# Another order of seven block products, one weight-sum buffer, and the first products on an unnormalised x, in the MLPs of a two-layer trunk

## The chip, the cores and the metric

The kernel runs on one core of a Trainium2 chip. The metric is the device time of one execution in microseconds.

## What is computed

A trunk of two layers on x (512 tokens, width 1024), all in fp32. Layer 0 mixes tokens by windowed attention, layer 1 by a recurrent block; both add a cross-attention on a memory. Each layer ends in the MLP that the change is about:

```python
x = x + jnp.concatenate([mixed, mo], axis=-1) @ w_out[l]
x = x + squared_relu_mlp(rms_norm(x, mlp_norm[l]), w_up[l], w_down[l])
# rms_norm:          x * rsqrt(mean(x*x) + EPS) * g
# squared_relu_mlp:  square(relu(h @ w_up)) @ w_down      (w_up 1024x4096, w_down 4096x1024)
```

## The kernel before, in words

x lies transposed in SBUF (xT, eight tiles of 128 features by 512 tokens). A product of fp32 values is made of three matmuls on high and low halves: high·high, high·low, low·high (L407, L409, L411). Each weight tile of 128x1024 comes as `raw` from memory (SP's queue, L102), ScalarE casts it to the high half `wh` (L352) and VectorE subtracts to get the low half `wl` (L353). There are four buffers each of wh and wl.

`mlp(l)` (L427) treats the hidden width in four groups of 1024. A step u*g* makes one group of w_up's product, a step d*g* takes one group through w_down and adds the result to xT. The order is u0 u1 d0 u2 d1 u3 d2, then d3 in layer 0; layer 1 ends with a plain product instead (`emit_last`). Each step is a 2x2 block product made with seven block products instead of eight (`seven`, L391), in the order of `PRODUCTS`. A step works on two quads (halves of the output blocks); for each product and quad there are 24 matmuls of 128x256, so a step has 336.

The weight operands of the seven products are blocks a11, a12, a22 and sums of them (`Quad.operand`, L333). The sums s3 and s1 are formed by a second, accumulating DMA from POOL's queue into a raw tile (L328). VectorE adds a22 to s3 into a tile `wsum` (L343, for product 6) and later a12 to it (L346, for product 3). Raw and wsum tiles of a Quad share a ring of RAWS = 8 buffers (a12, and a11 in the first step, use two others). The activation operands (`factor`, L368) are blocks of the input or sums of them, split into halves (L135, L136; for product 6 L378, L379) and kept in `h7` (seven buffers, made once for all u steps) or `u7` (two buffers, d steps). The results of products are added up in three PSUM banks per quad: x takes products 1, 6, 5, 3, y takes 2, z takes 7 and 4. In a d step VectorE adds each result from its bank to xT (L488), in a u step ScalarE and VectorE form the outputs and their squared ReLU (L458 to L473).

At the start of `mlp` the squares of x are summed while w_out's last products still run (`add_square`), then TensorE sums over partitions (`ps_ss`, L169), VectorE and ScalarE form 1/rms (L173 to L178), VectorE spreads it on a diagonal (`dg`, L158), TensorE broadcasts it (`ps_bc`, L160), and VectorE writes x·g/rms into blocks b (L439), from which the factors come.

Each engine runs its instructions in one fixed order. A scheduler sets it when the program is built, from the order of the code and the priorities given by `ahead(n)`; buffers that come free set the waits.

Of the kernel before, what the change touches and what calls it, by code (L numbers as in the profile page):

```python
# [60 lines left out]
def trunk(ctx: ExitStack, tc, xT_d, memT_d, wts_d, cols_d, ident_d, mask_d, pos_d, sink_d, outT_d, out_d, order):  # L61
# [302 lines left out]
    def activations(pool, room, tag, b, bufs):  # L364

        b[0] = room.tile([128, 4, 256], F32, tag="b0", name="b0", bufs=1)

        def factor(i, fine=False):  # L368
            t = pool.tile([128, 2, 4, 256], F32R, tag=tag, name=tag, bufs=bufs)
            src = b[{1: 11, 6: 0, 7: 12, 5: 11, 3: 22, 2: 21, 4: 0}[i]]  # L370
            with ahead(AHEAD_T):
                if i == 4:
                    V.tensor_tensor(out=b[0], in0=b[0], in1=b[21], op=ALU.subtract)
                for k in (((0, 2), (2, 4)) if i == 1 else ((0, 4),)):
                    k = slice(*k)
                    h, l, x = t[:, 0, k], t[:, 1, k], src[:, k]
                    if i == 6:
                        A.activation(out=h, in_=x, func=AF.Copy, scale=-1.0)  # L378
                        V.scalar_tensor_tensor(out=l, in0=x, scalar=-1.0, in1=h.bitcast(F32), op0=ALU.mult,  # L379
                                               op1=ALU.subtract)  # L380
                    else:
                        split((h, l), x)
# [8 lines left out]
    def seven(quads, factor, taken):  # L391
# [3 lines left out]
        for i in PRODUCTS:  # L395
            t = factor(i)
            for q, w in enumerate(quads):
                wh, wl = w.operand(i)
                if i in (1, 2, 7):
                    {1: x, 2: y, 7: z}[i][q] = seven_bank()  # L400
# [1 line left out]
                for p in range(2):
                    out = bank[:, p * 256:(p + 1) * 256]
                    for k in range(4):
                        c = slice((p * 4 + k) * 128, (p * 4 + k + 1) * 128)
                        first, last = i in (1, 2, 7) and p == 0 and k == 0, p == 1 and k == 3
# [552 lines left out]
```

## Time and profile before

| | |
|---|---|
| median of 3 runs | 1252.86 us (1249.09 to 1253.36) |
| profiled execution | 1252.73 us, span 1251.0 us |
| TensorE busy | 1177.0 us, 94% of the span |
| VectorE busy | 997.6 us, 80% |
| ScalarE busy | 767.4 us, 61% |
| mean granted TensorE clock | 0.969 |

The table is read from the top: the profiled execution is one of the same kind as the runs, its span is the time from its first to its last instruction, and the engines' busy times lie beside each other in it. Busy times over the whole span say little of one stage; the rows further below are of single stages.

### The profile page before, as it was taken

What the parts mean: (1) busy time and instruction counts of PE and PEld (TensorE: products, weight loads), DVE (VectorE), ACT (ScalarE), POOL (GpSimd) and SP (SyncE); (2) the same over time, 40 slices, a digit from 0 to 9 for tenths busy, and PEclk for the clock granted to TensorE, in tenths of its full rate; (3) what the DMA queues carried; (4) which work ended last, traced back from release to release, by engine and by line L of the source; (5) the groups of instructions that cost most, each with busy time, mean ns of one, the idle gap of its engine ahead of it and who ended that gap; (6) DMA issues with size and microseconds to landing.
All of it is one profiled execution on the core that took longest, in us unless ns stands there. A gap on an engine that the chain in (4) does not pass through costs nothing.

```text
span 1251.0 us, 20268 instructions
## 1 busy us (share of the span) xinstructions
PE 1177.0 (94%) x8084; PEld 1079.9 (86%) x8084; DVE 997.6 (80%) x1425; ACT 767.4 (61%) x1199; POOL 53.4 (4%) x69
## 2 busy tenths in 40 slices
PE   6999999996998999998999999999789999989997
PEld 6888888875898999998998877777589999989997
DVE  7978999766768968978987679997678687886954
ACT  7684598734665565574456789883377646646632
POOL 0000000001000100010000000001000100011000
PEclk9999999996998999998989999999799999999999
DMA  7412101125765677577233122238045676667131
GB/s 251 156 52 84 68 34 35 51 100 136 216 184 152 160 215 184 163 194 202 52 124 112 59 93 84 102 113 236 22 152 160 178 203 176 177 138 218 51 102 68
DMA packets 48910, 164.44 MB, mean 131 GB/s; under 512 B 5552, under 2 KB 9008, under 8 KB 48816
## 3 DMA queue, kind: packets, MB, share of 16 engines
q1 hardware_dynamic: 39456, 130.90, 30.8%
q0 software_dynamic: 8640, 31.46, 14.0%
q8 instruction: 63, 1.03, 0.3%
q10 hardware_dynamic: 720, 0.79, 0.2%
q14 instruction: 31, 0.25, 0.1%
HBM read 161.04 MB, written 2.10 MB: 130 GB/s over the span
## 4 chain that ended last, share of the span: by engine, by line
PE 66%; DVE 18%; DMA 8%; ACT 5%; issue 3%; SPq 0%; DVEq 0%; POOLq 0%; ACTq 0%
PE ps L409 10%; PE ps L411 10%; PE ps L407 10%; DMA raw<-wts 8%; DVE wl L353 4%; PE ps_o L118 3%; PE ps_o L119 3%; PE ps_o L120 3%; DVE xT L488 2%; PE sc L712 2%; PE pt L732 1%; DVE wl L114 1%; ACT wh L352 1%; PE pv L118 1%; PE ps_mq L119 1%
## 5 line engine op out<-in xcount | busy, mean ns | idle before, releaser
L407 PE MATMUL ps<-h,wh 128*128 128x256 f32 x896 | 251.6, 282 | 13.8 <-ACT h L135 11.5
L411 PE MATMUL ps<-h,wl 128*128 128x256 f32 x896 | 250.6, 281 | 4.5 <-DVE wl L353 4.5
L409 PE MATMUL ps<-h,wh 128*128 128x256 f32 x896 | 251.3, 281 | 1.7 <-DVE h L136 1.7
L352 ACT CAST wh<-raw 128x1024 fp32r<-128x1024 f32 x150 | 156.5, 1048 | 149.3 <-PE ps L409 129.8
L409 PE MATMUL ps<-u,wh 128*128 128x256 f32 x784 | 225.1, 287 | 10.3 <-DVE u L379 6.5
L407 PE MATMUL ps<-u,wh 128*128 128x256 f32 x784 | 224.2, 286 | 10.2 <-DVE xT L488 9.4
L411 PE MATMUL ps<-u,wl 128*128 128x256 f32 x784 | 223.9, 286 | 1.2 <-DVE wl L353 1.2
L353 DVE TENSOR_TENSOR wl<-raw,wh 128x1024 fp32r<-128x1024 f32 x150 | 182.1, 1219 | 46.8 <-ACT wh L352 46.4
L407 PEld LDWEIGHTS ps<-h,wh 128*128 128x128 f32 x896 | 171.4, 192 | 18.1 <-ACT h L135 15.1
L411 PEld LDWEIGHTS ps<-h,wl 128*128 128x128 f32 x896 | 170.3, 191 | 5.1 <-DVE wl L353 5.1
L409 PEld LDWEIGHTS ps<-h,wh 128*128 128x128 f32 x896 | 171.0, 191 | 2.5 <-DVE h L136 2.5
L407 PEld LDWEIGHTS ps<-u,wh 128*128 128x128 f32 x784 | 154.0, 197 | 11.2 <-DVE xT L488 10.0
L409 PEld LDWEIGHTS ps<-u,wh 128*128 128x128 f32 x784 | 153.3, 196 | 11.8 <-DVE u L379 7.1
L411 PEld LDWEIGHTS ps<-u,wl 128*128 128x128 f32 x784 | 153.0, 195 | 1.6 <-DVE wl L353 1.6
L113 ACT CAST wh<-raw 128x1024 fp32r<-128x1024 f32 x88 | 92.2, 1047 | 67.9 <-DMA raw<-wts 19.2
L114 DVE TENSOR_TENSOR wl<-raw,wh 128x1024 fp32r<-128x1024 f32 x88 | 107.1, 1217 | 24.5 <-ACT wh L113 24.2
L328 POOL DMA_DIRECT2D raw<-wts x60 | 52.0, 867 | 1103.0 <-DMA raw<-wts 850.1
L352 ACT CAST wh<-wsum 128x1024 fp32r<-128x1024 f32 x60 | 62.6, 1049 | 58.2 <-PE ps L409 52.2
L353 DVE TENSOR_TENSOR wl<-wsum,wh 128x1024 fp32r<-128x1024 f32 x60 | 72.9, 1220 | 23.1 <-ACT wh L352 22.8
L343 DVE TENSOR_TENSOR wsum<-raw 128x1024 f32<-128x1024 f32 x30 | 36.7, 1223 | 47.1 <-DMA raw<-wts 33.7
L488 DVE TENSOR_TENSOR xT<-xT,ps 128x512 f32<-128x512 f32 x98 | 66.0, 679 | 1.9 <-PE ps L411 1.5
L472 ACT ACTIVATE b<-b 128x512 f32<-128x512 f32 x48 | 30.1, 630 | 43.5 <-DVE b L470 43.5
(276 smaller groups left out, 2677.2 us busy)
## 6 DMA issues: line engine op xcount, KB each, us to landing
raw<-wts SPq DMA_DIRECT2D x238, 512.0 KB, 3.7
raw<-wts POOLq DMA_DIRECT2D x60, 512.0 KB, 7.7
mraw<-memT SPq DMA_DIRECT2D x16, 128.0 KB, 4.1
xT<-xT SPq DMA_DIRECT2D x8, 256.0 KB, 4.8
outT<-xT SPq DMA_DIRECT2D x8, 128.0 KB, 1.8
out<-fo ACTq DMA_DIRECT2D x2, 256.0 KB, 2.5
out<-fo SPq DMA_DIRECT2D x2, 256.0 KB, 2.7
posi<-pos SPq DMA_DIRECT2D x1, 256.0 KB, 5.6
```

Source lines behind the costliest of these rows:

```text
L113: A.copy(out=h, in_=raw)
L114: V.tensor_tensor(out=l, in0=raw, in1=h.bitcast(F32), op=ALU.subtract)
L118: T.matmul(out, lhsT=lhsT[0], rhs=rhs[0], start=start, stop=False)
L119: T.matmul(out, lhsT=lhsT[0], rhs=rhs[1], start=False, stop=False)
L120: T.matmul(out, lhsT=lhsT[1], rhs=rhs[0], start=False, stop=stop)
L328: P.dma_start(out=t, in_=wts_d[fetch_n[0]], accum_op=ALU.add)
L352: A.copy(out=h, in_=raw)
L353: V.tensor_tensor(out=l, in0=raw, in1=h.bitcast(F32), op=ALU.subtract)
L407: T.matmul(out, lhsT=wh[:, c], rhs=t[:, 0, k], start=first, stop=False, skip_group_check=True)
L409: T.matmul(out, lhsT=wh[:, c], rhs=t[:, 1, k], start=False, stop=False, skip_group_check=True)
L411: T.matmul(out, lhsT=wl[:, c], rhs=t[:, 0, k], start=False, stop=last, skip_group_check=True)
L488: V.tensor_tensor(out=dst, in0=dst, in1=src, op=ALU.add if n < 20 else ALU.subtract)
```

## The change

Products 7 and 6 change places. The tile s3 is kept as one sum `s`, to which a22 is added in place ahead of product 6 and a12 ahead of product 3; there is no wsum tile, and RAWS is 6. The factor sums are made each with its factor, u7 has three buffers, and the separate priority of the first step's weights (AHEAD_F) is gone. In u0 products 1 and 2 run on x·g without 1/rms: their operands `hx` take two of the h7 buffers and are made as soon as a tile of xT is done. Their results are multiplied by 1/rms (bc) afterwards: product 1's copies `p1` at L477, then added into the outputs (L486), products 1 and 2's sum at L513. x·g/rms is still written for the other factors, in 16 halves (L455) instead of 8 whole rows, and dg lies in b0's room.

```diff
-RAWS = 8
+RAWS = 6
-PRODUCTS = (1, 2, 6, 7, 5, 3, 4)
+PRODUCTS = (1, 2, 7, 6, 5, 3, 4)
...
         def operand(self, i):
             a = self.a
-            with ahead(AHEAD_F if self.first and i not in (1, 2) else AHEAD_W):
+            with ahead(AHEAD_W):
                 if i == 1:
                     a[11] = self.load((0, 0))
                 elif i == 2:
-                    a[12], a["s3"] = self.load((0, 1)), self.load((0, 0), (1, 0))
+                    a[12], a["s"] = self.load((0, 1)), self.load((0, 0), (1, 0))
+                elif i == 7:
+                    a[22] = self.load((1, 1))
                 elif i == 6:
-                    a[22], a["s1"] = self.load((1, 1)), self.load((1, 0), (1, 1))
-                    a["n"] = self.pool.tile([128, 1024], F32, tag="raw", name="wsum")
-                    V.tensor_tensor(out=a["n"], in0=a["s3"], in1=a[22], op=ALU.add)
-                op = split_raw(a[{1: 11, 6: "n", 7: "s3", 5: "s1", 3: "n", 2: 12, 4: 22}[i]])
-                if i == 6:
-                    V.tensor_tensor(out=a["n"], in0=a["n"], in1=a[12], op=ALU.add)
-            return op
+                    a["s1"] = self.load((1, 0), (1, 1))
+                if i in (6, 3):
+                    V.tensor_tensor(out=a["s"], in0=a["s"], in1=a[22 if i == 6 else 12], op=ALU.add)
+                return split_raw(a[{1: 11, 6: "s", 7: "s", 5: "s1", 3: "s", 2: 12, 4: 22}[i]])
...
-                if i == 1:
-                    V.tensor_tensor(out=b[11], in0=b[11], in1=b[12], op=ALU.subtract)
-                    V.tensor_tensor(out=b[0], in0=b[22], in1=b[11], op=ALU.add)
-                    V.tensor_tensor(out=b[12], in0=b[22], in1=b[12], op=ALU.subtract)
+                if i in (7, 6, 5, 4):
+                    t, x, y, op = {7: (12, 22, 12, ALU.subtract), 6: (0, 12, 11, ALU.add), 5: (11, 0, 22, ALU.subtract),
+                                   4: (0, 0, 21, ALU.subtract)}[i]
+                    V.tensor_tensor(out=b[t], in0=b[x], in1=b[y], op=op)
...
+    def product(i, quad, t, bank, start=None):
...
-    def seven(quads, factor, taken):
+    def seven(quads, factor, taken, left=False):
-        for i in PRODUCTS:
+        for i in PRODUCTS[2 if left else 0:]:
...
+            with ahead(AHEAD_E):
+                plain = [hm.tile([128, 2, 4, 256], F32R, tag="h7", name="hx", bufs=7) for _ in range(2)]
             for c in range(KD):
+                with ahead(AHEAD_E):
+                    split_scaled(part(plain[c % 2], c // 2), xT[c][:, :256], col(C_MLP + 8 * l + c))
                 add_square(acc, xT[c], c == 0)
             bc = st.tile([128, S], F32, tag="bc", name="bc", bufs=1)
-            rstd_of(acc, S, bc)
-            for c in (0, 2, 4, 6, 1, 3, 5, 7):
-                two = [a.rearrange("p (t s) -> p t s", t=2) for a in (xT[c], bc)]
-                V.scalar_tensor_tensor(out=b[c % 2 + 1][:, :, c // 2], in0=two[0], scalar=col(C_MLP + 8 * l + c),
-                                       in1=two[1], op0=ALU.mult, op1=ALU.mult)
+            first = [Quad(rp, f"w_up{l}", 0, q * 4, True) for q in range(2)]
+            sums, start = [], []
+            for q in range(2):
+                start.append(seven_bank())
+                product(1, first[q], plain[0], start[q])
+                sums.append(st.tile([128, S], F32, tag="sq", name="p1"))
+                with ahead(AHEAD_E):
+                    A.copy(out=sums[q], in_=start[q])
+            room = up.tile([128, 4, 256], F32, tag="b0", name="dg", bufs=1)
+            rstd_of(acc, S, bc, dg=room.rearrange("p a b -> p (a b)")[:, :S].rearrange("p (a b) -> p a b", a=4))
+            for q in range(2):
+                product(2, first[q], plain[1], start[q], False)
...
+            def normalise(half):
+                with ahead(AHEAD_T + 100 * half):
+                    for c in range(KD):
+                        V.scalar_tensor_tensor(out=b[c % 2 + 1][:, half, c // 2], in0=xT[c][:, HALVES[half]],
+                                               scalar=col(C_MLP + 8 * l + c), in1=bc[:, HALVES[half]], op0=ALU.mult,
+                                               op1=ALU.mult)
...
                 if g == 0:
-                    for i in PRODUCTS:
+                    normalise(1)
+                    h_of(7)
+                    normalise(0)
+                    for i in (6, 1, 5):
+                        h_of(i)
+                    with ahead(AHEAD_T):
+                        r = bc[:, :256].rearrange("p (o t) -> p o t", o=1).to_broadcast([128, 2, 256])
+                        two = [a.rearrange("p (a t) -> p a t", a=2) for a in sums + start]
+                        for q in range(2):
+                            V.tensor_tensor(out=two[q], in0=two[q], in1=r, op=ALU.mult)
+                    for i in (3, 4, 2):
                         h_of(i)
...
+                    if g == 0 and i in (6, 5, 3):
+                        dst = b[{6: 21, 5: 22, 3: 12}[i]][:, k]
+                        V.tensor_tensor(out=dst, in0=bank, in1=two[q], op=ALU.add)
...
+                if g == 0:
+                    for q in range(2):
+                        u = b[11][:, q * 2:q * 2 + 2]
+                        V.scalar_tensor_tensor(out=u, in0=two[q + 2], scalar=0.0, in1=r, op0=ALU.max, op1=ALU.mult)
+                        A.activation(out=u, in_=u, func=AF.Square)
+                quads = first if g == 0 else [Quad(rp, f"w_up{l}", 0, g * 8 + q * 4) for q in range(2)]
+                seven(quads, h_of, taken, g == 0)
...
-                      activations(up, up, "u7", us.pop(g), 2), taken)
+                      activations(up, up, "u7", us.pop(g), 3), taken)
```

TensorE's order at the start of layer 0's MLP, before: w_out's last matmuls, the two of the 1/rms chain, then product 1 on normalised operands (h7).

```order
L119 MATMUL ps_o_2886<-o1_2003,wh_2868 128x512
L120 MATMUL ps_o_2886<-o1_2003,wl_2869 128x512
L169 MATMUL ps_ss_2939<-ones_76,acc_2915 128x1 x4
L160 MATMUL ps_bc_2958<-dg_2953,ones_76 128x512
L407 MATMUL ps_7_3005<-h7_2970,wh_3001 128x256
L407 MATMUL ps_7_3037<-h7_2970,wh_3033 128x256
L409 MATMUL ps_7_3005<-h7_2970,wh_3001 128x256
```

And now: the last rows of product 1's start and of product 2, on hx, around the two matmuls of the 1/rms chain, up to the first row of product 7.

```order
L394 MATMUL ps_7_2990<-hx_2916,wh_2993 128x256
L395 MATMUL ps_7_2990<-hx_2916,wh_2993 128x256
L396 MATMUL ps_7_2990<-hx_2916,wl_2994 128x256
L169 MATMUL ps_ss_3024<-ones_76,acc_2915 128x1 x4
L394 MATMUL ps_7_2990<-hx_2916,wh_2993 128x256
...
L395 MATMUL ps_7_2990<-hx_2917,wh_3083 128x256
L160 MATMUL ps_bc_3042<-dg_3023,ones_76 128x512
L396 MATMUL ps_7_2990<-hx_2917,wl_3084 128x256
...
L396 MATMUL ps_7_2990<-hx_2917,wl_3084 128x256
L394 MATMUL ps_7_3161<-h7_3120,wh_3164 128x256
```

27 product matmuls now stand ahead of ps_ss, 56 between it and ps_bc, and 13 behind that before the first matmul on normalised operands.

VectorE's order in layer 1 at the end of d1, before: the xT adds of product 5 (two per quad: banks 10817 and 11032, then 10849 and 11061), the splits (wl) of product 4's weights, and between them the sum for the next step, u3 (wsum).

```order
L488 TENSOR_TENSOR xT_79<-xT_79,ps_7_10817 128x2x256
L353 TENSOR_TENSOR wl_11215<-raw_10951,wh_11214 128x1024
L488 TENSOR_TENSOR xT_79<-xT_79,ps_7_11032 128x2x256
L343 TENSOR_TENSOR wsum_11417<-raw_11340,raw_11412 128x1024
L488 TENSOR_TENSOR xT_79<-xT_79,ps_7_10849 128x2x256
L353 TENSOR_TENSOR wl_11244<-raw_10988,wh_11243 128x1024
L488 TENSOR_TENSOR xT_79<-xT_79,ps_7_11061 128x2x256
L488 TENSOR_TENSOR xT_79<-xT_79,ps_7_10817 128x2x256
L136 TENSOR_TENSOR u7_11210<-b0_10802,u7_11210 128x1024
```

And now the same place (banks 10860, 10969 and 11000), and the first rows in which the next step's sums are added.

```order
L352 TENSOR_TENSOR wl_11233<-raw_10970,wh_11232 128x1024
L528 TENSOR_TENSOR xT_79<-xT_79,ps_7_10969 128x2x256
L528 TENSOR_TENSOR xT_79<-xT_79,ps_7_10860 128x2x256
L375 TENSOR_TENSOR b0_11747<-b1_10368 128x1024
L528 TENSOR_TENSOR xT_79<-xT_79,ps_7_11000 128x2x256
L352 TENSOR_TENSOR wl_11262<-raw_11001,wh_11261 128x1024
...
L352 TENSOR_TENSOR wl_11434<-raw_11359,wh_11433 128x1024
L345 TENSOR_TENSOR raw_11359<-raw_11359,raw_11431 128x1024
L352 TENSOR_TENSOR wl_11465<-raw_11396,wh_11464 128x1024
L345 TENSOR_TENSOR raw_11396<-raw_11396,raw_11462 128x1024
```

The a22 add (L345) of u3 now stands behind the splits of u3's own product 7 (wl_11434, wl_11465), each quad by itself; between the two splits of d1's product 4 there is only a sum of factors (L375) and xT adds.

SP's queue around the start of layer 0's MLP, before: w_out's last raw tile, then the MLP's. The wait of raw_3065 is for w_out's last matmul.

```order
L102 DMA raw_2866<-wts 128x1024 [waits DMAHW6_49,DVE_49]
L102 DMA raw_2999<-wts 128x1024 [waits DMAHW7_49,DVE_49]
L102 DMA raw_3031<-wts 128x1024 [waits DMAHW0_49,DVE_49]
L102 DMA raw_3063<-wts 128x1024 [waits DMAHW1_49,DVE_49]
L102 DMA raw_3100<-wts 128x1024 [waits DMAHW2_49,DVE_49]
L102 DMA raw_3065<-wts 128x1024 [waits PE_49]
L102 DMA raw_3102<-wts 128x1024
```

And now. The wait of raw_3047 is for the end of windowed attention (its last split, on VectorE, and matmul), those of raw_2958 and raw_2991 for the splits of w_out's last two tiles.

```order
L101 DMA raw_2866<-wts 128x1024 [waits DMAHW6_49,DVE_49]
L101 DMA raw_3047<-wts 128x1024 [waits DVE_49,PE_49]
L101 DMA raw_2958<-wts 128x1024 [waits DMAHW7_49,DVE_49]
L101 DMA raw_3080<-wts 128x1024
L101 DMA raw_3162<-wts 128x1024
L101 DMA raw_3193<-wts 128x1024
L101 DMA raw_2991<-wts 128x1024 [waits DMAHW0_49,DVE_49]
```

The first load in the MLP's ring no longer waits for w_out's last matmul.

## Rows read from the trace of the kernel before

**Rows 1.** The page: busy time of TensorE (share of the span, instructions), and by engine the shares of the chain that ended last.

```profile
PE 1177.0 (94%) x8084; PEld 1079.9 (86%) x8084; DVE 997.6 (80%) x1425; ACT 767.4 (61%) x1199; POOL 53.4 (4%) x69
PE 66%; DVE 18%; DMA 8%; ACT 5%; issue 3%; SPq 0%; DVEq 0%; POOLq 0%; ACTq 0%
```

**Rows 2.** Busy time of each engine in single block steps: the window (us from the span's start) and its length, then PE, PEld, DVE, ACT and POOL busy us (instructions), granted TensorE clock, share of the DMA engines, GB/s. In order: layer 0 u0, d0, d1, d2, d3; layer 1 u0, d0, u2, d1, d2.

```profile
294.62:342.88 48.26, 43.71 (x336) 42.61 (x337) 39.81 (x41) 29.79 (x40) 2.59 (x3) 0.91 0.56 148
381.20:427.51 46.31, 42.18 (x339) 41.59 (x337) 40.48 (x43) 24.57 (x28) 3.45 (x4) 0.93 0.64 177
467.08:510.88 43.80, 41.17 (x339) 40.97 (x337) 37.02 (x40) 22.16 (x24) 3.45 (x4) 0.96 0.66 170
548.96:596.00 47.04, 42.07 (x339) 41.65 (x337) 41.91 (x50) 25.58 (x33) 4.01 (x5) 0.93 0.72 188
596.00:636.50 40.50, 39.28 (x339) 38.47 (x338) 38.31 (x42) 21.46 (x22) 0.31 (x1) 1.00 0.23 63
899.97:945.77 45.80, 41.37 (x336) 40.28 (x337) 35.87 (x37) 28.19 (x38) 2.59 (x3) 0.95 0.48 142
985.38:1032.42 47.04, 42.95 (x339) 42.54 (x337) 40.59 (x43) 24.46 (x28) 3.45 (x4) 0.93 0.61 167
1032.42:1070.50 38.08, 38.08 (x339) 38.08 (x337) 27.98 (x28) 24.87 (x33) 3.45 (x4) 1.00 0.68 182
1070.50:1116.01 45.51, 40.94 (x339) 40.43 (x337) 38.91 (x42) 22.63 (x25) 4.31 (x5) 0.96 0.67 172
1155.58:1195.15 39.57, 39.57 (x338) 39.57 (x337) 38.11 (x45) 24.85 (x30) 0.86 (x1) 1.00 0.23 67
```

**Rows 3.** Waits of VectorE, TensorE and SP's queue over the whole span: who waited at which line for whom, us in total, times, longest.

```profile
DVE wsum L343 <- DMA raw<-wts: 33.7, 11, 6.8
PE ps L407 <- DVE xT L488: 9.4, 3, 4.6
PE ps L409 <- DVE u L379: 6.5, 3, 3.0
SPq L102 <- DVE wsum L346: 296.3, 30, 42.1
```

**Rows 4.** Timeline of layer 1 at d1's product 3, which follows product 5 in the same banks: start, duration (us), engine, line, operation, and the idle time before it with what ended it.

```profile
1098.08 0.68 DVE L488 TENSOR_TENSOR xT<-xT,ps 128x512 f32<-128x512 f32 x1
1098.14 0.28 PE L407 MATMUL ps<-u,wh 128*128 128x256 f32 x1
...
1101.09 0.28 PE L411 MATMUL ps<-u,wl 128*128 128x256 f32 x1
...
1104.05 1.23 DVE L343 TENSOR_TENSOR wsum<-raw 128x1024 f32<-128x1024 f32 x1 [5.29 <-DMA raw<-wts]
...
1105.93 0.58 PE L407 MATMUL ps<-u,wh 128*128 128x256 f32 x1 [4.56 <-DVE xT L488]
```

**Rows 5.** Timeline of layer 0 from w_out's last matmul to the first product; columns as in rows 4 (SPq: six DMA issues one after the other).

```profile
277.25 0.40 PE L120 MATMUL ps_o<-o,wl 128*128 128x512 f32 x1
277.68 2.84 SPq L102 DMA_DIRECT2D raw<-wts  x6
...
291.31 1.23 DVE L343 TENSOR_TENSOR wsum<-raw 128x1024 f32<-128x1024 f32 x1 [6.82 <-DMA raw<-wts]
...
294.62 0.79 PE L407 MATMUL ps<-h,wh 128*128 128x256 f32 x2 [7.94 <-ACT h L135]
```

**Rows 6.** The same stretch in layer 1.

```profile
887.83 0.39 PE L120 MATMUL ps_o<-ol,wl 128*128 128x512 f32 x1
...
890.25 0.68 DVE L149 TENSOR_TENSOR acc<-acc,sq 128x512 f32<-128x512 f32 x1
...
890.99 1.87 PE L169 MATMUL ps_ss<-ones,acc 128*128 128x1 f32 x8 [2.77 <-DVE acc L149]
...
894.13 0.87 DVE L158 TENSOR_SCALAR dg<-ident,r 128x128 f32<-128x128 f32 x4
...
899.97 0.80 PE L407 MATMUL ps<-h,wh 128*128 128x256 f32 x2 [2.77 <-ACT h L135]
```

**Rows 7.** Busy times as in rows 2, of the end of w_out in layer 0 and of the two stretches at half clock.

```profile
255.00:277.60 22.60, 22.60 (x99) 18.23 (x98) 14.28 (x18) 8.61 (x12) 0.00 (x0) 1.00 0.19 70
279.85:300.32 20.47, 9.15 (x33) 7.25 (x34) 11.22 (x23) 2.58 (x5) 3.63 (x4) 0.50 0.93 241
890.83:904.48 13.65, 7.95 (x27) 6.02 (x28) 8.43 (x20) 2.17 (x5) 0.00 (x0) 0.50 0.00 0
```

**Rows 8.** Groups of instructions by line: engine, operation, output and inputs, count, busy us, mean ns of one, idle us before.

```profile
L353 DVE TENSOR_TENSOR wl<-raw,wh 128x1024 fp32r<-128x1024 f32 x150 | 182.1, 1219 | 46.8 <-ACT wh L352 46.4
L140 DVE SCALAR_TENSOR_TENSOR memH<-mraw,cols,memH 128x256 fp32r<-128x256 f32 x16 | 7.0, 479 | 0.7 <-ACT memH L139 0.6
L139 ACT ACTIVATE memH<-mraw,cols 128x256 fp32r<-128x256 f32 x16 | 7.1, 498 | 0.7 <-DMA mraw<-memT 0.5
L352 ACT CAST wh<-raw 128x1024 fp32r<-128x1024 f32 x150 | 156.5, 1048 | 149.3 <-PE ps L409 129.8 <-PE ps_o L119 9.3 <-DVE wl L353 6.2
```

**Rows 9.** DMA issues of raw weights on SP's queue (count, KB, median us to landing), and the accumulating ones of line 328 on POOL's: ns of one issue (min/median/max, start of the first and last), and min/median/max us to landing.

```profile
raw<-wts SPq DMA_DIRECT2D x238, 512.0 KB, 3.7
L328 POOL DMA_DIRECT2D raw<-wts x60: 862/862/1005, 281.7 to 1156.0; - x60
DMA to landing us min/median/max: 5.0/7.7/11.5
```

More of the change, by code (lines that the diff above doesn't have):

```diff
@@ L366, in activations, with factor @@
         b[0] = room.tile([128, 4, 256], F32, tag="b0", name="b0", bufs=1)
-        def factor(i, fine=False):
-            t = pool.tile([128, 2, 4, 256], F32R, tag=tag, name=tag, bufs=bufs)
+        def factor(i):
             src = b[{1: 11, 6: 0, 7: 12, 5: 11, 3: 22, 2: 21, 4: 0}[i]]
             with ahead(AHEAD_T):
[L372 to L382, printed above, removed]
-                if i == 1:
-                    V.tensor_tensor(out=b[11], in0=b[11], in1=b[12], op=ALU.subtract)
-                    V.tensor_tensor(out=b[0], in0=b[22], in1=b[11], op=ALU.add)
-                    V.tensor_tensor(out=b[12], in0=b[22], in1=b[12], op=ALU.subtract)
-            return t
@@ L389, in activations @@
-        return factor
-    def seven(quads, factor, taken):
+                f = pool.tile([128, 2, 4, 256], F32R, tag=tag, name=tag, bufs=bufs)
+                if i in (7, 6, 5, 4):
+                    t, x, y, op = {7: (12, 22, 12, ALU.subtract), 6: (0, 12, 11, ALU.add), 5: (11, 0, 22, ALU.subtract),
+                                   4: (0, 0, 21, ALU.subtract)}[i]
+                    V.tensor_tensor(out=b[t], in0=b[x], in1=b[y], op=op)
+                if i == 6:
+                    A.activation(out=f[:, 0], in_=src, func=AF.Copy, scale=-1.0)
+                    V.scalar_tensor_tensor(out=f[:, 1], in0=src, scalar=-1.0, in1=f[:, 0].bitcast(F32), op0=ALU.mult,
+                                           op1=ALU.subtract)
+                else:
+                    split(part(f), src)
@@ new lines, in factor @@
+            return f
+        return factor
+    def product(i, quad, t, bank, start=None):
+        wh, wl = quad.operand(i)
+        for p in range(2):
+            out = bank[:, p * 256:(p + 1) * 256]
+            for k in range(4):
+                c = slice((p * 4 + k) * 128, (p * 4 + k + 1) * 128)
+                first = (i in (1, 2, 7) if start is None else start) and p == 0 and k == 0
+                T.matmul(out, lhsT=wh[:, c], rhs=t[:, 0, k], start=first, stop=False, skip_group_check=True)
+                T.matmul(out, lhsT=wh[:, c], rhs=t[:, 1, k], start=False, stop=False, skip_group_check=True)
+                T.matmul(out, lhsT=wl[:, c], rhs=t[:, 0, k], start=False, stop=p == 1 and k == 3,
+                         skip_group_check=True)
@@ L394, in seven @@
+    def seven(quads, factor, taken, left=False):
         x, y, z = {}, {}, {}
-        for i in PRODUCTS:
+        for i in PRODUCTS[2 if left else 0:]:
             t = factor(i)
[L397 to L400, printed above, removed]
+            for q, quad in enumerate(quads):
+                if i in (1, 2, 7) or left and i == 6:
+                    {1: x, 2: y, 7: z, 6: x}[i][q] = seven_bank()
@@ L401, in seven @@
                 bank = (x if i in (1, 6, 5, 3) else y if i == 2 else z)[q]
[L402 to L406, printed above, removed]
-                        T.matmul(out, lhsT=wh[:, c], rhs=t[:, 0, k], start=first, stop=False,
-                                 skip_group_check=True)
-                        T.matmul(out, lhsT=wh[:, c], rhs=t[:, 1, k], start=False, stop=False,
-                                 skip_group_check=True)
-                        T.matmul(out, lhsT=wl[:, c], rhs=t[:, 0, k], start=False, stop=last,
-                                 skip_group_check=True)
+                product(i, quad, t, bank, left and i == 6 or None)
@@ L475, in emit_up @@
                 zs = {}
-                seven([Quad(rp, f"w_up{l}", 0, g * 8 + q * 4, g == 0) for q in range(2)], h_of, taken)
+                if g == 0:
[5 more added lines that the diff above has]
+                seven(quads, h_of, taken, g == 0)
             def emit_down(g):
```

12 lines of the change are left out of this document (8 added, 4 removed).

## The prediction

> **What bounds the kernel now.** I read the page first, then the busy times by step, then the waits, and last the two places where a block of products starts. TensorE is busy 94% of the span and makes 66% of the chain that ended last [rows 1], so time can only come from stretches in which it waits or runs slowly. The table by step [rows 2] shows where these are. The third step of layer 1 (u2) has 336 product matmuls in 38.08 us with TensorE busy throughout; its last block step (d2) has as many in 39.57 us, busy throughout too, at the same full clock. So a step without a stall costs 38.1 to 39.6 us, and which of the two it gets I cannot read off anything in the trace. Against that stand u0 with 48.26 and 45.80, the d steps of both layers with 43.80 to 47.04, and the pair d2, d3 of layer 0 with 87.54.
>
> The stalls of the d steps have one origin. VectorE waited 33.7 us for raw weights at L343, where it adds a22 to the sum s3; TensorE's longest waits in the products are for an xT add (9.4 us) and for a split factor of VectorE (6.5 us) [rows 3]. The timeline of one of them shows the link [rows 4]: at 1098.76 VectorE has done its xT add and stands at L343 until 1104.05, because that weight is still on its way. It serves its queue in order, so the next xT add and the low half of the next weight stand behind; TensorE's matmuls go on at 0.1135 us apiece (27 from 1098.14 to 1101.09) and then it idles 4.56 us. The load is late because SP's queue, which is in order too, waited 296.3 us in 30 waits for L346 to be done with a buffer [rows 3].
>
> At the start of each MLP the last w_out matmul is issued at 277.25 and at 887.83, and the first product matmul at 294.62 and at 899.97 [rows 5, 6]. In between TensorE has only the sum of squares and the broadcast of 1/rms, and its granted clock falls to 0.50 and stays there to 300.32 and to 904.48, inside u0 [rows 7]. In layer 0 the raw loads are issued only at 277.68, and VectorE then waits 6.82 us at L343 for one of them [rows 5].
>
> **The change, part by part.** *Order of products and one sum.* Products 7 and 6 swap, so a22 is needed one product (5.44 us, 38.08/7) later, and the a22 add no longer stands in the queue ahead of the previous step's work: in the new order it comes behind the splits of its own step's product 7. The adds are as many as before (two per quad, 1.22 us each, as the split [rows 8]), so VectorE's work is the same and only its place moves. A raw load takes 3.7 us and an accumulating load 7.7 us [rows 9]; by the new chain of buffers the sum's accumulate starts about three products before its use, which leaves some 7 us. I take the waits of L343 as gone.
>
> What is late next in a d step is VectorE itself: 40.48 and 40.59 us of work in d0 against 38.08 of products [rows 2]. But the first factors (two splits of 1.22 us and an add of the same size) now stand in the u step before, where VectorE has 28 of 38 us to do [rows 2], since a third factor buffer lets them. That leaves it 37 to 38 us in d0, about as much as TensorE; I allow 0.7 us of stall in each d step. A step then takes 38.8 (midway between the two paces) + 0.7 = 39.5 us. Layer 0: d0 46.31 - 39.5 = 6.8, d1 43.80 - 39.5 = 4.3. Layer 1: d0 47.04 - 39.5 = 7.5, d1 45.51 - 39.5 = 6.0, d2 39.57 stays. d2 and d3 of layer 0 follow each other without a u step; VectorE's 41.91 + 38.31 = 80.2 us is the floor there, I take 82.5, gain 87.54 - 82.5 = 5.0. Sum 29.6 us.
>
> *Six raw buffers for eight.* One sum buffer for two tiles pays for them. It costs nothing as long as the margin of 7 us above holds; if it does not, the wait is back, at ScalarE's split (first rival).
>
> *The start, layer 1* [rows 6]. Two products on x·g need 96 matmuls, 10.9 us at full clock, from about 888.1. Their operands (eight times a split of 128x256: ScalarE 0.498, VectorE 0.479 us, as memH's [rows 8]) are made during w_out, where VectorE has 14.28 of 22.60 us to do [rows 7], so I cost these 3.8 us at nothing; without that cover they would be 3.8 us on the path. The 1/rms chain runs beside: acc is done at 890.93 as before, and ps_ss stands behind 27 product matmuls in the queue. VectorE now also has the splits and sums of the first weights between the links of that chain (four of 1.22 us), which moves dg from 894.1 to about 899; ps_bc ends at 900.2, product 2 at 901.65, bc at 900.9. For product 7 then nine 128x256 normalisations (0.45 back to back), a p1 multiply (0.68, as an xT add [rows 4]) and the factor's sum (1.2) follow on VectorE to 907.2, and ScalarE's cast (1.05) to 908.3. So TensorE idles 6.6 us. The five products left take 27.2 us; after such an idle stretch the trace shows half clock (0.50) [rows 7], in which a product takes up to twice as long, and I charge 4 us for that. VectorE, with the other factors to make, is late once more at product 5: 2.7 us. (Today's u0 loses 45.80 - 38.08 = 7.7 us to these two things.) End of u0: 908.3 + 27.2 + 4 + 2.7 = 942.2, now 945.77 (899.97 + 45.80): gain 3.6 us.
>
> *The start, layer 0.* The chain is the same, 610.5 us earlier, so u0 ends at 331.7; now it ends at 342.88. The gain is 11.2 us, since the wait for loads goes as well: in the new order the first loads wait for the end of windowed attention and for w_out's splits, not for w_out's last matmul, and are in memory when the products start.
>
> *The sum.* 29.6 + 3.6 + 11.2 = 44.4 us off the profiled execution's 1252.73 us (span 1251.0), which is within 0.2 us of the median of 1252.86: 1208.3 us. **Bounds of what I cannot see:** fifteen steps all at the fast pace (38.08) or all at the slow one (39.57) move it by 11 us either way. The d steps gain at least nothing and at most down to 38.08 each: 29.6 becomes 0 or 35.7. The start of layer 1 has, at worst, VectorE late for every factor (8 us lost instead of 3.6 gained), at best no half clock (7.6 gained).
>
> **Rivals.** *The wait moves.* With six buffers the accumulating loads land late (they take up to 11.5 us), ScalarE waits at the split for product 7, and TensorE behind it as now. For it: 296 us of SP's waits [rows 3] show how tight buffers are. Against: one tile per quad fewer is in use. Only the starts gain then: 1252.7 - 14.8 = 1238. Chance 0.12. On the same transfers, the Trainium skill's page "SBUF — State Buffer", section "Who interferes with whom" (and its note on DVE blocking DMA), says that a VectorE instruction that holds the shared port pair keeps GpSimd from writing descriptors, so more VectorE work in u0 would delay GpSimd's loads. By that rule it would come to this rival's time. The sixty such issues of the trace take 0.86 us each, 1.0 at most [rows 9], and show no such delay, so of the chance above no more than 0.03 is for this way.
>
> *The start does not pay.* VectorE's chain between bc and the factors is longer than I have it, and u0 stays at today's ends; 1252.7 - 29.6 = 1223. Chance 0.15.
>
> *Slower: the chain on one bank.* Products 6, 5, 3 now follow each other in the same PSUM bank of each quad, and VectorE adds from that bank between them. TensorE may start 5 on quad 0 only when the add of 6 is done, and has one quad's 24 matmuls (2.72 us) for it; before, only 3 after 5 was so. These are four waits in each of seven d steps and two u0, 36 in all. With the gain of 44.4, it turns at 1.2 us per wait, that is, if the add ends 3.9 us after the product on the mean; at 1.5 us the time is 1252.7 - 44.4 + 54 = 1262. For it: 9.4 us of today's waits are of this kind [rows 3], and VectorE is the fullest engine of a d step. Against: all three of these came while VectorE stood at L343 [rows 4]. Chance 0.07.
>
> *Nothing moves.* The stalls come from elsewhere and are only renamed: about 1252, chance 0.06.
>
> **The numbers.** The forecast has 0.60: 1208.3 us. The range reaches up to the first rival, 1238, and down to 1194: all d stalls gone (6.1 us more) and ten steps or so at the fast pace (8 us). Slower rival and no change lie outside, with half of the first rival and a little below. A measurement of this kernel tells about 0.5% (6 us) from no change. Faster: 0.60 + 0.12 + 0.15 = 0.87; same 0.06; slower 0.07.
>
> **What would show it.** Right: no wait of VectorE for raw weights at the sum's line beyond a microsecond or two; d steps of 39 to 41 us; TensorE busy within half a microsecond of w_out's end, then one gap of 5 to 8 us ahead of product 7 at half clock; u0 ending near 332 in layer 0 and 54 us after w_out in layer 1. Wrong: ScalarE waiting for raw at product 7 (first rival); product 7's gap over 10 us (second); TensorE's first matmul of products 5 and 3 waiting for xT adds by over a microsecond each (third).

## The result, and the profile after

Four runs of the changed kernel have a median of 1202.36 us (1194.98 to 1205.16), beside 1250.97 us for the kernel before; the ratio is 0.9608 with a 95% interval of 0.9553 to 0.9662. 1208.3 us had been forecast. The profiled execution took 1205.16 us, 47.6 us less than that of before.

The page, the same two lines as [rows 1]: busy time by engine, and the chain that ended last.

```profile
PE 1157.5 (96%) x8084; PEld 1065.1 (89%) x8084; DVE 1013.7 (84%) x1464; ACT 767.2 (64%) x1194; POOL 53.3 (4%) x69
PE 75%; DVE 17%; ACT 3%; DMA 3%; issue 2%; SPq 0%; DVEq 0%; ACTq 0%
```

TensorE does the same matmuls in 19.5 us less busy time, with a mean granted clock of 0.987 (0.969 before), and 28 us in which it stood idle are gone. DMA fell from 8% of the chain to 3%.

The steps, with the columns of [rows 2]: layer 0 u0, d0, d1, d2, d3, then layer 1 u0, d0, u2, d1, d2. u0 begins with w_out's end now, as its first two products do.

```profile
277.50:331.35 53.85, 44.43 (x348) 42.69 (x346) 50.96 (x71) 30.93 (x39) 0.86 (x1) 0.94 0.30 92
370.92:410.49 39.57, 39.57 (x338) 39.57 (x337) 38.35 (x41) 21.96 (x23) 3.46 (x4) 1.00 0.67 180
450.07:489.64 39.57, 39.57 (x338) 39.57 (x337) 38.35 (x41) 21.95 (x23) 3.45 (x4) 1.00 0.67 178
529.21:572.94 43.73, 41.42 (x338) 40.86 (x337) 37.78 (x43) 24.64 (x31) 3.45 (x4) 0.96 0.65 171
572.94:613.28 40.34, 39.30 (x338) 38.51 (x336) 39.64 (x46) 19.20 (x21) 1.72 (x2) 1.00 0.34 94
865.43:919.92 54.49, 44.99 (x347) 43.45 (x346) 50.80 (x71) 31.11 (x39) 1.72 (x2) 0.91 0.29 94
958.00:996.12 38.12, 38.12 (x339) 38.12 (x337) 37.23 (x40) 22.30 (x24) 3.45 (x4) 1.00 0.71 194
996.12:1034.20 38.08, 38.08 (x339) 38.08 (x337) 29.40 (x29) 25.42 (x34) 3.45 (x4) 1.00 0.74 205
1034.20:1072.32 38.12, 38.12 (x338) 38.12 (x337) 37.23 (x40) 22.28 (x24) 3.45 (x4) 1.00 0.68 184
1110.40:1148.91 38.51, 38.33 (x338) 38.16 (x337) 37.84 (x43) 22.99 (x28) 1.72 (x2) 1.00 0.35 98
```

In the d0 and d1 steps TensorE is busy from end to end in both layers, where each took 4 to 9 us longer before. VectorE's work fell in d0, from 40.5 us to 38.4 in layer 0 and from 40.6 to 37.2 in layer 1, but in layer 0's d1 it rose, from 37.0 to 38.4, and the stall went all the same. The two a22 adds of the next u step no longer lie in the d step; its own two now do. Before, three such adds of 1.22 us lay in each d0, one its own and two of u2. So it is their place that changed, far more than the amount of VectorE's work. u0 ends 53.7 us after w_out's end in layer 0 (65.2 before) and 54.3 in layer 1 (57.6 before).

What is waited for now, as [rows 3]: TensorE's waits in the products, VectorE's one wait for raw weights, and SP's wait for the sums.

```profile
PE ps L394 <- ACT h L134: 12.1, 2, 6.1
PE ps L395 <- DVE h L135: 6.3, 4, 2.5
PE ps L396 <- DVE wl L352: 1.8, 1, 1.8
PE ps L394 <- DVE xT L528: 1.0, 3, 0.5
DVE wl L352 <- DMA raw<-wts: 0.5, 1, 0.5
ACT wh L351 <- DMA raw<-wts: 3.4, 5, 0.9
SPq L101 <- DVE raw L345: 283.7, 30, 22.0
```

The 33.7 us of VectorE at L343 are gone: at the sum's line (L345) it waits for no load. Elsewhere 0.5 us of VectorE and 3.4 us of ScalarE are left, and no wait of TensorE in the products is put down to a cast of weights. Nearly all that is left of TensorE's waits (the first two lines) is in the two u0. SP still waits 284 us for sums, so the total of such waits was not the evidence for tight buffers that the first rival took it for.

The start in layer 1, to be read beside [rows 6]: TensorE around the broadcast, at product 7 and at product 5.

```profile
876.62 1.10 PE L160 MATMUL ps_bc<-dg,ones 128*128 128x512 f32 x2 [0.33 <-DVE dg L158]
...
885.30 0.58 PE L394 MATMUL ps<-h,wh 128*128 128x256 f32 x1 [6.09 <-ACT h L134]
...
901.98 0.39 PE L395 MATMUL ps<-h,wh 128*128 128x256 f32 x1 [2.43 <-DVE h L135]
```

VectorE meanwhile, between the broadcast and factor 7, and before product 5:

```profile
877.64 1.23 DVE L345 TENSOR_TENSOR raw<-raw 128x1024 f32<-128x1024 f32 x1
878.78 3.65 DVE L455 SCALAR_TENSOR_TENSOR b<-xT,cols,bc 128x256 f32<-128x256 f32 x9
882.35 0.68 DVE L477 TENSOR_TENSOR p<-p,bc 128x512 f32<-128x512 f32 x1
882.95 1.22 DVE L375 TENSOR_TENSOR b<-b,b 128x1024 f32<-128x1024 f32 x1
...
899.56 4.63 DVE L135 TENSOR_TENSOR h<-b,h 128x1024 fp32r<-128x1024 f32 x4
```

The nine normalisations and the p1 multiply stand between the broadcast and the sum that product 7 needs, and before product 5 goes on (901.98) VectorE is at four splits in a row, of which it needs the second. Two stretches at half clock follow the gaps (columns as in [rows 7]).

```profile
882.93:889.76 6.83, 3.81 (x16) 3.52 (x17) 6.83 (x13) 1.04 (x1) 0.00 (x0) 0.50 0.00 0
903.41:906.83 3.42, 3.42 (x18) 3.42 (x18) 3.27 (x5) 0.00 (x0) 0.00 (x0) 0.50 0.02 5
```

### The profile page after: what moved, and what is told of

The parts are those of the page before. It is cut to its first block, busy times and chain, and to the rows that moved or that the text cites. A ratio compares the mean times of both kernels' runs of the same rounds, so it can differ in the third digit from the quotient of the medians.

```text
span 1203.4 us, 20324 instructions
## 1 busy us (share of the span) xinstructions
PE 1157.5 (96%) x8084; PEld 1065.1 (89%) x8084; DVE 1013.7 (84%) x1464; ACT 767.2 (64%) x1194; POOL 53.3 (4%) x69
## 4 chain that ended last, share of the span: by engine, by line
PE 75%; DVE 17%; ACT 3%; DMA 3%; issue 2%; SPq 0%; DVEq 0%; ACTq 0%
PE ps L395 13%; PE ps L394 13%; PE ps L396 13%; DVE wl L352 3%; PE ps_o L117 3%; PE ps_o L119 3%; PE ps_o L118 3%; DMA raw<-wts 2%; DVE xT L528 2%; PE sc L752 2%; PE pt L772 1%; DVE wl L113 1%; PE pv L117 1%; PE ps_mq L118 1%; PE ps_q L119 1%
## 5 line engine op out<-in xcount | busy, mean ns | idle before, releaser
L351 ACT CAST wh<-raw 128x1024 fp32r<-128x1024 f32 x210 | 219.1, 1048 | 178.1 <-PE ps L395 120.7
L352 DVE TENSOR_TENSOR wl<-raw,wh 128x1024 fp32r<-128x1024 f32 x210 | 254.9, 1217 | 60.5 <-ACT wh L351 59.7
L394 PE MATMUL ps<-h,wh 128*128 128x256 f32 x832 | 234.3, 282 | 12.1 <-ACT h L134 12.1
L395 PE MATMUL ps<-h,wh 128*128 128x256 f32 x832 | 234.4, 282 | 6.3 <-DVE h L135 6.3
L396 PE MATMUL ps<-h,wl 128*128 128x256 f32 x832 | 233.7, 281 | 0.0
L394 PEld LDWEIGHTS ps<-h,wh 128*128 128x128 f32 x832 | 158.7, 191 | 12.7 <-ACT h L134 12.5
L395 PEld LDWEIGHTS ps<-h,wh 128*128 128x128 f32 x832 | 158.4, 190 | 7.3 <-DVE h L135 7.3
L394 PEld LDWEIGHTS ps<-u,wh 128*128 128x128 f32 x784 | 148.0, 189 | 2.0 <-issue 1.7
L395 PEld LDWEIGHTS ps<-u,wh 128*128 128x128 f32 x784 | 147.9, 189 | 0.8 <-DVE u L135 0.8
L112 ACT CAST wh<-raw 128x1024 fp32r<-128x1024 f32 x88 | 92.0, 1047 | 62.8 <-DMA raw<-wts 32.2
L113 DVE TENSOR_TENSOR wl<-raw,wh 128x1024 fp32r<-128x1024 f32 x88 | 106.9, 1216 | 28.8 <-ACT wh L112 28.5
L345 DVE TENSOR_TENSOR raw<-raw 128x1024 f32<-128x1024 f32 x60 | 73.0, 1219 | 0.8
L134 ACT CAST u<-b 128x1024 fp32r<-128x1024 f32 x42 | 43.9, 1049 | 14.3 <-PE ps L396 8.3
L135 DVE TENSOR_TENSOR u<-b,u 128x1024 fp32r<-128x1024 f32 x42 | 50.9, 1212 | 0.0
L217 DVE TENSOR_TENSOR xT<-xT,ps_o 128x512 f32<-128x512 f32 x48 | 32.6, 679 | 7.8 <-PE ps_o L119 7.5
```

Source lines behind the costliest of these rows:

```text
L112: A.copy(out=h, in_=raw)
L113: V.tensor_tensor(out=l, in0=raw, in1=h.bitcast(F32), op=ALU.subtract)
L135: V.tensor_tensor(out=dst[1], in0=src, in1=dst[0].bitcast(F32), op=ALU.subtract)
L345: V.tensor_tensor(out=a["s"], in0=a["s"], in1=a[22 if i == 6 else 12], op=ALU.add)
L351: A.copy(out=h, in_=raw)
L352: V.tensor_tensor(out=l, in0=raw, in1=h.bitcast(F32), op=ALU.subtract)
```

## The experiments

All are variants of the changed kernel. Times of u0 are counted from the end of w_out's last matmul to the first matmul of u1, so that kernels with different starts compare; 65.2 and 57.6 us before, 53.7 and 54.3 after, layers 0 and 1. Ratios are to the kernel before in the same group of runs; its medians were 1246.37, 1241.33 and 1242.16 us. Line numbers are those of each variant's own file.

**One half of the change each.** First without the start on x:

```diff
-            with ahead(AHEAD_W):
+            with ahead(40 if self.first and i not in (1, 2) else AHEAD_W):
...
-            first = [Quad(rp, f"w_up{l}", 0, q * 4, True) for q in range(2)]
...
+            rstd_of(acc, S, bc)
+            for c in (0, 2, 4, 6, 1, 3, 5, 7):
...
-                seven(quads, h_of, taken, g == 0)
+                seven([Quad(rp, f"w_up{l}", 0, g * 8 + q * 4, g == 0) for q in range(2)], h_of, taken)
```

> The new order of products, the one sum and the third factor buffer stay; the start on x without 1/rms is undone (rstd first, whole-row normalisation, product 1's factor in halves, as in the kernel before). Theory (the terms add, the d steps gain by the order alone): the d and u1 to u3 steps run without stalls of VectorE at the sum's line, as in the changed kernel (38.1 to 39.6 us each), so some 34 us of the 48.6 stay: about 1217 us, with layer 1's u0 ending 57 to 58 us after w_out as before. Rival 1 (the gain of layer 0's start comes from the loads, not from the start on x): u0 of layer 0 also ends 5 to 7 us earlier than before, about 1210 us. Rival 2 (the early start gives the loads the lead that the later steps live on): the waits for raw weights are back and it is 1230 us or more.

1216.85 us, ratio 0.9776 (0.9745 to 0.9807). The main theory held for the d steps: layer 1's d0, d1 and both of layer 0 have no stall.

```profile
966.13:1004.26 38.13, 38.13 (x339) 38.13 (x337) 37.24 (x41) 22.36 (x25) 3.46 (x4) 1.00 0.71 190
1042.34:1080.86 38.52, 38.52 (x338) 38.52 (x337) 37.63 (x42) 22.37 (x25) 3.46 (x4) 1.00 0.69 189
```

u0 took 60.9 us in layer 0, 4.3 less than before (rival 1, in kind), and 60.5 in layer 1, 2.9 more. In both TensorE waited for a split of product 7's weights (4.8 and 4.6 us of this row):

```profile
PE ps L397 <- DVE wl L352: 9.9, 4, 4.8
```

Then the start alone, in the old order:

```diff
-PRODUCTS = (1, 2, 7, 6, 5, 3, 4)
+PRODUCTS = (1, 2, 6, 7, 5, 3, 4)      # and wsum, RAWS = 8, two u7 buffers, as before
```

> Old order of products (1 2 6 7 5 3 4), a separate wsum tile, eight raw buffers and two factor buffers as before, with the start on x without 1/rms. Theory: u0 gains as in the changed kernel (11.4 us in layer 0, 3.2 in layer 1, measured from w_out's end) and the d steps keep their stalls of 4 to 8 us: about 1236 us. Rival (the start on x pays in layer 0 only where the loads come early, which the new order and sum bring): layer 0's u0 gains under 5 us, about 1243 us.

1236.17 us, ratio 0.9918 (0.9887 to 0.9948). The time is the forecast one by luck: 14.6 us of gain were meant and 10.2 came, and the parts are others. Layer 0's u0 took 67.9 us, more than before, layer 1's 54.7. Both d0 kept their stalls (46.0 and 45.8 us), but d1 took only 42.4 and 41.8, and layer 0's d2 42.3 (47.0 before). In layer 0 VectorE stands at the old sum again, and the factors stand behind it:

```profile
291.70 1.23 DVE L343 TENSOR_TENSOR wsum<-raw 128x1024 f32<-128x1024 f32 x1 [7.34 <-DMA raw<-wts]
...
305.01 0.58 PE L403 MATMUL ps<-h,wh 128*128 128x256 f32 x1 [14.20 <-ACT h L386]
```

So the start on x gains nothing in layer 0 unless the loads come early (the rival was right, and by more than it said), and the two halves are not a sum there: -2.6 alone, 4.3 for the other half alone, 11.5 together. (The first half has six raw buffers here and the second eight, which the runs below show to matter.)

**The order alone, and the buffers.** Two sum tiles again in the new order:

```diff
-RAWS = 6
+RAWS = 8
...
-                if i in (6, 3):
-                    V.tensor_tensor(out=a["s"], in0=a["s"], in1=a[22 if i == 6 else 12], op=ALU.add)
...
+                if i == 6:
+                    a["n"] = self.pool.tile([128, 1024], F32, tag="raw", name="wsum")
+                    V.tensor_tensor(out=a["n"], in0=a["s"], in1=a[22], op=ALU.add)
...
-                      activations(up, up, "u7", us.pop(g), 3), taken)
+                      activations(up, up, "u7", us.pop(g), 2), taken)
```

> Order 1 2 7 6 5 3 4 and the start on x as in the changed kernel, but with the sum in two tiles again (raw s and wsum), eight raw buffers and two factor buffers. Theory (it is the order: the a22 add leaves the end of the step before): no stall at the a22 add in any step, 1202 to 1210 us, as with one sum. Rival (it is the one sum: only with fewer tiles in the ring do the loads come early enough): waits for raw weights of 20 us or more in all are back and it is 1220 to 1235 us.

1208.75 us, ratio 0.9732 (0.9667 to 0.9796). Its d0 and d1 steps run without any stall in both layers, here layer 1's:

```profile
957.39:995.48 38.09, 38.09 (x339) 38.09 (x338) 37.14 (x40) 22.26 (x24) 3.71 (x5) 1.00 0.75 197
1033.56:1071.63 38.07, 38.07 (x338) 38.07 (x337) 37.13 (x40) 22.24 (x24) 2.81 (x4) 1.00 0.70 190
```

It is the order that frees the d steps (with it the a22 load, which is now asked for at product 7): start_only has the same number of buffers and sum tiles in the old order, and stalls. But layer 0's u0 took 64.3 us. Next the third factor buffer:

```diff
-                      activations(up, up, "u7", us.pop(g), 3), taken)
+                      activations(up, up, "u7", us.pop(g), 2), taken)
```

> As the changed kernel, with two u7 factor buffers instead of three. Theory (the third buffer lets the first two factors of a d step be made in the u step before and the third one a product earlier): VectorE's work comes back into the d steps, each d step stalls 1 to 3 us, and 1207 to 1220 us results. Rival (order and place of the sums are all): no d step stalls more than now, 1202 us, same.

1206.53 us, ratio 0.9689 (0.9649 to 0.973). The rival was right: d0 took 39.57 and 38.53 us without a stall, and VectorE's 38.35 us in layer 0's d0 are those of the changed kernel. Two buffers leave room for more raw tiles; eight and seven, to be read beside u7_two, which has six, and with three factor buffers five:

```diff
-RAWS = 6
+RAWS = 8      # raws_eight, two u7 buffers;  7: raws_seven, two u7 buffers;  5: raws_five, three u7 buffers
```

> As the changed kernel, with eight raw buffers and two factor buffers (the third factor buffer takes the room of two raw ones). With five buffers TensorE waited 62 us for splits that waited for raw weights, with six and two factor buffers ScalarE 10.5 us in seven waits and TensorE none of it. Theory (six is the edge, just enough): ScalarE's waits for raw weights fall below 3 us, TensorE's time stays, 1202 to 1208 us. Rival (the loads still cost something with six): it is faster than the changed kernel by over 3 us in step lengths without the pace.

1218.65 us, ratio 0.9801 (0.9741 to 0.9861): worse than with six. Layer 0's u0 (first line) took 65 us, layer 1's 56.

```profile
277.80:342.85 65.05, 48.22 (x348) 45.85 (x347) 53.42 (x73) 32.79 (x41) 6.23 (x7) 0.84 0.65 191
872.61:928.53 55.92, 46.27 (x348) 44.74 (x347) 51.51 (x71) 31.54 (x40) 2.59 (x3) 0.88 0.36 103
```

The loads show why. With eight buffers POOL's first accumulating load of layer 0 is issued after w_out's end, and SP's queue waits 8.5 us for w_out's last matmul (first fence, where the second line has us, times, longest); in the changed kernel (second fence) it is issued 26 us earlier.

```profile
282.34 1.91 POOL L328 DMA_DIRECT2D raw<-wts  x2 [280.41 <-PE ps_ss L169]
SPq L101 <- PE ps_o L119: 8.5, 1, 8.5
```

```profile
256.64 1.00 POOL L328 DMA_DIRECT2D raw<-wts  x1 [254.71 <-DVE xT L217]
```

> As the changed kernel, with seven raw buffers and two factor buffers. With eight, layer 0's u0 took 65.0 us, with six 53.7 to 55.6. Theory (with eight the pool of raw tiles lies partly on the room of w_out's operands and its loads wait for w_out's last matmul; seven still lie beside it): layer 0's u0 takes 54 to 56 us and no step waits for raw weights: 1203 to 1207 us. Rival (it is not the room but the loads of more buffers that crowd the start): layer 0's u0 takes about 60 us, 1210 us.

1208.96 us, ratio 0.9687 (0.9601 to 0.9774), u0 53.9 us in layer 0 and 53.4 in layer 1.

```profile
278.01:332.08 54.07, 44.56 (x348) 42.85 (x347) 50.47 (x71) 30.51 (x39) 1.73 (x2) 0.91 0.33 90
```

The edge lies between seven and eight: each of the four kernels with eight raw buffers (before, start_only, order_alone, raws_eight) has the 8.5 us wait of SP's queue for w_out's last matmul, and none of the others has it. By the program the first sum's tile then has the room of w_out's operand o1; the traces show the wait, not the room. Then five:

> As the changed kernel, with five raw buffers instead of six. It prices the margin of the loads, which I put at some 7 us with six. Theory (margin of 7 us, about one load's lead of one and a half products): one buffer fewer takes about one product (5.4 us) of lead per quad, the loads still come in time in the u steps and are late by a few us at some d steps: 1205 to 1225 us. Rival 1 (no margin left with six): waits for raw weights in nearly every step, above 1230 us. Rival 2 (the loads are far ahead): 1202 us, same.

1289.81 us, ratio 1.0359 (1.0321 to 1.0397), slower than the kernel before: rival 1. Every step waits at product 5, whose sum comes by the accumulating load:

```profile
358.60 0.86 POOL L328 DMA_DIRECT2D raw<-wts  x1 [16.21 <-DMA raw<-wts]
363.91 2.00 ACT L351 CAST wh<-raw 128x1024 fp32r<-128x1024 f32 x2 [7.08 <-DMA raw<-wts]
...
365.01 0.58 PE L394 MATMUL ps<-h,wh 128*128 128x256 f32 x1 [6.08 <-ACT wh L351]
```

24 such waits make 62.3 us of TensorE's time. ScalarE's waits for raw weights went from 3.4 us in five (six buffers) to 86.5 us in 24, so six hold the loads just in time.

```profile
PE ps L394 <- ACT wh L351: 62.3, 24, 6.1
ACT wh L351 <- DMA raw<-wts: 86.5, 24, 7.1
```

Last, both tiles of the sum with seven buffers, the edit of order_alone with `RAWS = 7`:

> The new order and the start on x with two sum tiles (s and wsum), seven raw buffers and two factor buffers. With eight raw buffers this kernel ran d steps of 38.08 us, but layer 0's u0 took 64.5. Theory (order is all; the one sum only saves room): layer 0's u0 takes 54 to 57 us and the d steps stay without stalls, 1200 to 1206 us. Rival (with seven buffers two tiles for the sum are one too many, as with five buffers and one): splits wait for raw weights in each step, above 1220 us.

1212.28 us, ratio 0.975 (0.9662 to 0.9838). The d0 and d1 steps stay without stalls (38.08 in layer 0, 39.57 in layer 1); layer 0's u0 took 58.7 us, more than the theory had. VectorE's longest wait for raw weights at the sum, 5.3 us, lies ahead of w_out's end, and 53.4 us of its work fall into this u0 (50.5 with one sum and seven buffers); that the one comes from the other is not shown. So the one sum is worth room, and some 5 us of layer 0's u0 at seven buffers.

**The yardstick and a better start.** The changed kernel unaltered:

> The changed kernel unaltered, as the yardstick of this group. Both theories expect its earlier time, 1202 us within the spread of its runs (1195 to 1205), and the same stalls. It is also a second trace for the matmul pace: if a pace of 0.1133 or 0.1177 us per matmul lasts until TensorE is held up once, the steps between two hold-ups have one length, 38.08 or 39.57 us, but not necessarily the one that they had in the first trace.

1203.88 us, ratio 0.9697 (0.9633 to 0.976). The kernel before had 1241.33 us in this group and 1250.97 in the first, so the change is worth 37 us here and 49 there, and the ratios of the two groups differ by about 1%. u0 took 53.5 and 55.5 us. Layer 0's d0 took 38.12 us here and 39.57 in the first trace, layer 1's 39.58 here and 38.12 there, at full clock and with TensorE busy throughout in all four:

```profile
369.20:407.32 38.12, 38.12 (x338) 38.12 (x337) 37.23 (x40) 22.28 (x24) 3.46 (x4) 1.00 0.72 191
952.29:991.87 39.58, 39.58 (x339) 39.58 (x338) 38.36 (x41) 21.95 (x23) 3.46 (x4) 1.00 0.70 181
```

Then VectorE's order at the start:

```diff
-        with ahead(AHEAD_R):
+        with ahead(soon):      # 400 in mlp
...
-            src = b[{1: 11, 6: 0, 7: 12, 5: 11, 3: 22, 2: 21, 4: 0}[i]]
+            src = b[{1: 11, 6: 0, 7: 12, 5: 12, 3: 22, 2: 21, 4: 0}[i]]
...
-                    h_of(7)
+                    with ahead(100):
+                        h_of(7)
                     normalise(0)
-                    for i in (6, 1, 5):
+                    for i in (6, 5):
...
-                    for i in (3, 4, 2):
+                    for i in (3, 4, 1, 2):
...
-                if step == "d2" and extra2:
-                    extra2()
...
                 emit_down(3)
+                if extra2:
+                    extra2()
```

> The changed kernel with three things more: the chain of 1/rms ahead of the splits of product 7's weights; factor 7's sum ahead of the p1 multiplies and factors 5 and 6 ahead of those of products 1 and 2, which later steps need (the sum for 5 goes into b12's room so that factor 1 may wait); layer 1's memory split after d3 instead of after d2. Theory (what is left at the starts is VectorE's order, and the d2 stall of layer 0 is ScalarE waiting for the memory loads in its queue): the gap ahead of product 7 falls from 6.1 to about 4 us, the one at product 5 (2.5 us) goes, the starts gain 3 to 6 us each and layer 0's d2, d3 about 4 us: 1188 to 1194 us. Rival (the starts are bound by the number of VectorE instructions, not by their order): starts unchanged, 1198 us.

1202.65 us, ratio 0.9686 (0.963 to 0.9742). The gap ahead of product 7 fell to 4.2 us, the one at product 5 became a new one, and u0 stayed at 54.2 and 54.2: TensorE now waits for the add of product 6's result, which stands behind five splits.

```profile
PE ps L394 <- ACT h L134: 8.5, 2, 4.2
PE ps L394 <- DVE b L487: 6.3, 2, 3.1
```

Layer 0's d2 and d3 gained about 2 us instead of 4 (d2 took 42.5): the scheduler still put ScalarE's part of the memory split into d2, so what the d2 stall is due to was not tested. Then, with all of v_all kept, the four factors that are not needed at once were taken out of the queue (against v_all):

```diff
-                    for i in (3, 4, 1, 2):
-                        h_of(i)
```

> As v_all, but factors 3, 4, 1 and 2 of the u steps are made when the products that use them come, not all ahead: in v_all the add of product 6's result stood in VectorE's queue behind five such splits, and TensorE waited 3.1 us for it in each u0. Theory (u0 is bound by what stands on VectorE ahead of the add): that wait goes, u0 falls from 54.3 to 50 or 51 us in both layers, 1196 us. Rival (VectorE's work in u0 as a whole is the bound, the wait moves to the next factor): u0 stays at 54, 1203 us.

1201.49 us, ratio 0.9636 (0.9564 to 0.9709). The wait for the add is gone and u0 took 50.0 and 50.5 us, as the theory had it, 3.5 to 5 us shorter in each layer than in the two traces of the changed kernel. But VectorE also has less to do inside u0 (47.1 and 47.3 us, 50.5 and 50.2 in v_all), so the run does not tell the place of the splits from their number:

```profile
278.25:328.40 50.15, 44.11 (x347) 42.39 (x346) 47.12 (x68) 29.04 (x37) 1.73 (x2) 0.93 0.33 97
854.22:904.90 50.68, 45.11 (x348) 43.63 (x346) 47.31 (x68) 29.50 (x38) 1.72 (x2) 0.93 0.33 95
```

The medians do not separate it from the changed kernel (1202.36 and 1203.88); only the u0 steps show the gain. Its profiled execution ran from layer 0's u2 on mostly at the slow pace; how the other runs went is not shown.

## Why the prediction was right, and where it was not

*The d steps.* Forecast: the waits at L343 go, 39.5 us a step. Measured: 39.57 twice in layer 0, 38.12 twice in layer 1, no stall. The step that carried it, the a22 add leaving the previous step's queue, is shown: order_alone has it with two sum tiles and two factor buffers, and start_only, which lacks it, has the stalls. That 39.57 meets 39.5 in layer 0 is luck: the 0.7 us of stall that were allowed did not come, and the pace was the slow one. Layer 0's d2 and d3 took 84.1 us where 82.5 were forecast, with a wait of 1.8 us for a split in d2 (L352) and a granted clock of 0.96 there. Between the two profiled executions layer 0's u1 to d3 went from 293.6 to 281.9 us and layer 1's u1 to d2 from 249.4 to 229.0: 32.1 us in all, forecast 29.6.

*The third factor buffer* was said to move VectorE's work into the u step. That was wrong: u7_two has the same d steps, and d0 holds six splits of factors after the change as before. Nor was VectorE's work what had to fall: layer 0's d1 has more of it now and no stall.

*Six raw buffers* were said to leave some 7 us. Wrong, though it cost nothing: ScalarE already waited for raw weights five times (3.4 us), and with one buffer fewer the kernel is slower than before. The first rival was one buffer away; that six sufficed was in part luck.

*The starts.* Layer 1's u0 was to end 54.1 us after w_out and did after 54.3, with gaps of 6.1 and 2.4 us where 6.6 and 2.7 were forecast; from w_out's end on, the broadcast, the factor's sum and ScalarE's cast for product 7 ended within 0.5 us of where the chain had them. 7.2 us of busy time lay at half clock, 3.6 lost, where 4 were charged. Layer 0's was to end at 331.7 and did at 331.35. Its reason was right in that the loads must come early, but that belonged to the number of raw tiles (raws_eight: 64.9 us, raws_seven: 53.9), and the start on x without it costs 2.6 us.

*The rivals.* "The start does not pay" did not come, nor did the chain on one bank in the d steps: TensorE waited 1.0 us for xT adds in all. The chain is real, however: in v_all's u0 it cost 3.1 us per layer, as soon as five splits stood ahead of the add. Nor were GpSimd's loads held up: its sixty issues took 0.86 us at the median and 1.0 at most, as before, and landed in 7.4 us (7.7 before). But only one or two of them lie in a u0, where VectorE's work grew.

*The sum.* 47.6 us between the two executions, forecast 44.4: 11.5 + 3.2 at the starts (11.2 + 3.6), 32.1 in the steps (29.6), and 0.8 elsewhere. Its largest error, layer 0's steps 4.4 us less than forecast and layer 1's 6.9 more, is for the most part the pace, which the prediction had as a bound of 11 us and which no run explains. Between medians the gain was 48.6 us in the first group and 37.5 in the second, so part of the closeness is luck. Two of the prediction's sums are off by 0.4 us, without weight: 900.9 and the three terms behind it end at 906.8, not 907.2, and 29.6 with four d steps at 38.08 becomes 35.3, not 35.7.

## What to carry to other kernels

When an engine that serves its queue in order waits for a load, look at which step the waiting instruction belongs to: here an add for the next step stood among the previous step's work, and moving its use by one product freed the d steps with eight buffers as with six. The number of buffers in a ring has two edges, one where loads come too late (five) and one where, by the program, the pool reaches into room that is still in use (eight); both cost 10 us and more. The total of the load queue's waits for the sum does not show the first (284.9 us with five, 283.7 with six); what tells the two is a cast that waits for an accumulating load, and a load that waits for the last matmul of the stage before. A start that takes an operation off the critical path pays only if its operands are there; test it alone and with the other half.

## What the runs showed that was not expected

Matmuls of 128x256 run one after the other at 0.1133 or at 0.1178 us apiece (38.08 and 39.57 us for 336), at the same full clock and with the same instructions. In these traces a pace lasts for whole steps until TensorE is held up once, by a gap or a hold-up of a few tenths of a microsecond, and may be the other one after it; neither layer, step nor kernel decides which (after_again). Over fifteen steps that is up to 22 us, more than the difference of most variants here. Whether it also makes the spread between runs of one kernel is not shown, since one execution of each was traced. What sets it stays open.
